# A hybrid attention block on one core: shared transposes of reciprocal sums, values by heads, modulation rows as columns

## The chip, the cores and the metric

The kernel runs on one core of a Trainium2 chip. A core has a matrix engine (TensorE, PE), a vector engine (VectorE, DVE), an activation engine (ScalarE, ACT), GpSimd (POOL), a sync engine (SyncE, SP) that issues all DMAs here, and 16 DMA engines. The metric is the device time of one execution in microseconds (us): the median of several.

## The reference

One layer of a diffusion trunk over 1024 latent tokens (16 rows of 64) and 256 context tokens, width 1024, all in float32. Cut to what matters:

```
m, mc = split(silu(c) @ w_ada + b_ada, 9), split(silu(c_ctx) @ w_ada + b_ada, 9)
x     = x     + 0.5 * m[2]  * rms(swiglu(rms(x)*(1+m[1])+m[0]))        # feed-forward 1
h_ctx = h_ctx + 0.5 * mc[2] * rms(swiglu(...))
qa, ka, va, cq, ckv, kr, gates = split(modnorm(x, m[3], m[4]) @ w_in)  # and of h_ctx
o_na  = neighbourhood_attention(qa, ka, va, ka_ctx, va_ctx, rpb)       # 8 heads of 64, 8x16 windows
q, k, v = up-projections of rms(cq), rms(ckv); rotary on 32 of 96 columns
o_mla = softmax(q k^T / sqrt(96)) v                                    # 8 heads over 1280 keys
y     = sigmoid(gates) * (o_na @ w_o_na, o_mla @ w_o_mla), summed, @ w_out
x     = x + m[5] * rms(y);   x = x + 0.5 * m[8] * rms(swiglu(modnorm(x, m[6], m[7])))
```

## The kernel before

A float32 product is made of three matmuls of two rounded parts: every operand is split into a high half (ScalarE's cast) and a low half (VectorE's subtract), and `mm3` (line 152) sums high x high, high x low and low x high. The feed-forwards and the projections of gates, queries and keys go by *units* (`Unit`): 1024 x 256 of weights against 1024 x 1024 of activations in seven block products of 12 matmuls of 512 columns (the names p3 to p7 in the code), whose sums VectorE makes. The planes of activations are made by `Planes.fill0` and `fill1`: four transposes of 128 x 128 by TensorE, then two ScalarE evictions or one and a VectorE copy, then a VectorE subtract.

The order of work is written out. A `Plan` (line 157) has a list of main steps, mostly one block product each, and side steps hung on them by `spread`; within one slot, side steps run in the order in which they were hung. Every instruction of these parts is kept in this order on its engine. A store is issued some steps after its data (`store`, `flush`), all by SyncE's one queue.

Stages in order of time: the first feed-forward, whose first planes were made without the shift (`shift_planes` adds it later, around 50 us); its down-projection; the normalise chains (`chain1`) and the second set of planes (`fill0s`, from 894 us); the units of gates, queries and keys (to about 1180); the latent projections and the values (`va_tile`, 1262 to 1318), which stores the values for the four column blocks `vws[j]` of the neighbourhood attention; the up-projections (`kv_heads`, with `rotate` for the keys; `q_heads`); then 64 attention *items*: 32 of the neighbourhood attention (head by head, four column blocks each, from 1418 us), 32 of the latent attention (head by head, four blocks of 256 queries, to 1824). Then the merge (`wo_step`), `out_tile` and the second feed-forward. The modulation rows m[2] to m[8] are formed alongside by `AdaSum` (line 271): VectorE multiplies and adds the weights as they arrive, and `add_up` sums the 128 partitions by matmuls with a one-pick column, copies the rows out, and `turn` transposes them into columns.

An item makes scores three items ahead, its softmax (line 1500 or 1598) one or two ahead, then transposes the probabilities (line 150, cast at 1520 or 1622, subtract at 1521 or 1623), and multiplies them with the values (`weigh`). `head_out` (line 1449) ends it: the reciprocals of the sums of exponentials, one column per 128 queries, are spread over 128 columns and transposed by TensorE into rows, ScalarE copies one half of the product (line 1456) and these rows (1457), VectorE adds the other half (1458), and GpSimd multiplies and splits (1459 to 1462).

Of the kernel before, what the change touches and what calls it, by code (L numbers as in the profile page):

```python
# [15 lines left out]
P = 128  # L16
# [27 lines left out]
def hybrid_block(ctx: ExitStack, tc: tile.TileContext, a: dict, out: bass.AP):  # L44
# [98 lines left out]

    vec, act, pool = Engine(nc.vector), Engine(nc.scalar), Engine(nc.gpsimd)
# [12 lines left out]
    class Plan:  # L157
# [113 lines left out]
    class AdaSum(Ada):  # L271
# [30 lines left out]
    def ada_steps(ms):  # L302
# [12 lines left out]
        def end(m):  # L315
            cur[m].turn()
# [5 lines left out]
        for m in ms:  # L322
            s += [lambda m=m, k=k, h=h: step(m, k, h) for k in range(KD + 1) for h in range(2)]
            s += [lambda: None, lambda m=m: cur[m].add_up(), lambda m=m: end(m)]
# [481 lines left out]
    def shift_planes(ks):  # L806
        for k in ks:
# [5 lines left out]
            act.activation(t, t, AF.Identity, bias=mod[0][:, 0, k:k + 1])  # L813
# [203 lines left out]
    def emit_q(i, ci, x, bank):  # L1017
# [11 lines left out]
    def emit_k(i, c0, n, x):  # L1029
        hi, lo = T2(F32R)[:, :n], T2(F32R)[:, :n]  # L1030
        split_to(hi, lo, x)
        store(kas[i][0, :, c0:c0 + n], f32(hi))
        store(kas[i][1, :, c0:c0 + n], f32(lo))

    punits = []
    for p in list(range(4, 12)) + [0, 1, 2, 3]:
# [4 lines left out]
        elif p < 4:  # L1041
            punits.append(Unit(h2, srcs, lambda i, ci, x, bank, i0=i0: emit_k(i0 - 4 + i, ci * 512, 512, x)))
# [6 lines left out]
    plan_chains(plan, pos, 2, chain1)  # L1049

# [4 lines left out]
    plan.spread([lambda k=k: fill0s()[k]() for k in range(KD)], pos[3] + 6, o + 2)  # L1055
# [53 lines left out]
    vws = [DR([4, P, D]) for _ in range(4)]  # L1109
    vcs = DR([NCTX, D])  # L1110
# [51 lines left out]
    def va_tile(s, t):  # L1162
# [5 lines left out]
        if t < 8:  # L1168
            for j in range(4):
                for r in range(2):  # L1170
                    row = 2 * t + r
                    o, q = 64 * r + KSTART[j], (row % 4) * 32
                    store(vws[j][row // 4, q:q + 32, :], f32(v[o:o + 32, :]))
        else:
            store(vcs[(t - 8) * P:(t - 7) * P, :], f32(v))
# [31 lines left out]
    def rotate(x, cc, ss, nh):  # L1207
# [11 lines left out]
        vec.tensor_tensor(x, v1, v2, op=ALU.add)  # L1219

# [54 lines left out]
    class NaHead:  # L1275


        def loads(self, h):
# [15 lines left out]
            for j in range(2):  # L1294
                self.values(va, j)
            yield
            ld(f32(kvc[:, 256:512]).rearrange("p (t c) -> p t c", t=2),
               vcs[:, h * P:(h + 1) * P].rearrange("(t p) c -> p t c", p=P))
# [150 lines left out]
    def head_out(pv, r, h, hi, lo, shape):  # L1449
# [12 lines left out]
        nc.gpsimd.tensor_tensor(lo[b:b + 64], o, f32(hi[b:b + 64]), op=ALU.subtract)  # L1462

# [7 lines left out]
    class NaItem:  # L1471
        def __init__(self, head, j):
            self.head, self.j = head, j

        def scores(self):
# [4 lines left out]
            m, n_, l, r = ST(4), ST(2), ST(2), ST(2)  # L1480
# [17 lines left out]
            self.r = r  # L1498
# [3 lines left out]
            soft.append(lambda: nc.vector.reciprocal(r, l))  # L1502
            yield
# [443 lines left out]
```

## Time and profile before

| | |
|---|---|
| median of 3 runs | 2685.34 us (2684.7 to 2686.59) |
| profiled execution: own time / span | 2686.6 / 2684.8 us |
| granted TensorE clock, mean | 0.996 of full |
| TensorE, VectorE, ScalarE, GpSimd busy | 98%, 69%, 43%, 8% |
| DMA | 409.43 MB, 152 GB/s mean |

A row of a timeline names the engine, the source line (L120 is the helper that pins every instruction, L147 the matmuls, L150 the transposes, L132 the DMAs), the operation and the tiles as out<-in: xu, xv, xy, xo and t are tiles of SBUF, w weights or attention operands, st statistics, bm, bs and bv banks of PSUM, d scratch in HBM, and in_ an input. Where several instructions of one kind follow each other they share a row (x4), and the bracket says how long the engine stood idle before the row and which engine's instruction ended that. A float32 matmul shows as several records where its operands are not rounded ones: one one-column product gives two.

### The profile page before, as it was taken

What the parts mean: (1) busy time and instruction counts of PE and PEld (TensorE: products, weight loads), DVE (VectorE), ACT (ScalarE), POOL (GpSimd) and SP (SyncE); (2) the same over time, 40 slices, a digit from 0 to 9 for tenths busy, and PEclk for the clock granted to TensorE, in tenths of its full rate; (3) what the DMA queues carried; (4) which work ended last, traced back from release to release, by engine and by line L of the source; (5) the groups of instructions that cost most, each with busy time, mean ns of one, the idle gap of its engine ahead of it and who ended that gap; (6) DMA issues with size and microseconds to landing.
All of it is one profiled execution on the core that took longest, in us unless ns stands there. A gap on an engine that the chain in (4) does not pass through costs nothing.

```text
span 2684.8 us, 37871 instructions
## 1 busy us (share of the span) xinstructions
PE 2627.2 (98%) x13820; PEld 2245.7 (84%) x13820; DVE 1845.9 (69%) x3488; ACT 1146.3 (43%) x2176; POOL 218.4 (8%) x348
## 2 busy tenths in 40 slices
PE   7999999999999999999999999999999999999998
PEld 5888888888888788799888999997788888888887
DVE  3777876586876676664558988885445777565776
ACT  5532223522233653331437888882256322324111
POOL 0000000000001300000102422220030000000001
PEclk9999999999999999999999999999999999999999
DMA  7444433453442664486789953205235433225323
GB/s 276 161 154 146 148 122 122 142 168 110 157 134 96 226 208 157 139 294 217 233 274 255 237 124 77 72 9 196 71 118 176 138 130 114 76 90 196 118 94 126
DMA packets 183194, 409.43 MB, mean 152 GB/s; under 512 B 21664, under 2 KB 59744, under 8 KB 183008
## 3 DMA queue, kind: packets, MB, share of 16 engines
q1 hardware_dynamic: 183008, 407.01, 46.9%
q8 instruction: 109, 1.79, 0.3%
q14 instruction: 77, 0.63, 0.1%
HBM read 307.77 MB, written 99.16 MB: 152 GB/s over the span
## 4 chain that ended last, share of the span: by engine, by line
PE 72%; issue 16%; DMA 5%; DVE 3%; ACT 2%; POOL 1%; SPq 0%; DVEq 0%; POOLq 0%; ACTq 0%
PE bs L147 32%; PE bm L147 20%; PE bv L147 16%; DMA w<-d 4%; PE bm L150 3%; DVE t L120 1%; ACT t L120 1%; ACT xu L120 1%; PE bs L150 1%; DVE xv L120 1%; DVE xu L120 1%; POOL st L120 1%; PE bv L150 0%; DMA xv<-in_wada 0%; ACT xv L120 0%
## 5 line engine op out<-in xcount | busy, mean ns | idle before, releaser
L147 PE MATMUL bm<-xu,xu 128*128 128x512 f32 (+2 forms) x2304 | 551.0, 388 | 4.1 <-ACT xu L120 3.3
L147 PEld LDWEIGHTS bm<-xu,xu 128*128 128x128 f32 x2304 | 424.9, 188 | 89.4 <-ACT xu L120 4.1
L147 PE MATMUL bs<-xu,xu 128*128 128x512 f32 (+1 forms) x1908 | 459.0, 386 | 1.4 <-DVE xu L120 0.9
L147 PEld LDWEIGHTS bs<-xu,xu 128*128 128x128 f32 x1908 | 354.1, 189 | 70.5 <-ACT xu L120 0.9
L147 PE MATMUL bs<-xv,xu 128*128 128x512 f32 (+1 forms) x1488 | 352.5, 386 | 3.9 <-DVE t L120 3.9
L147 PEld LDWEIGHTS bs<-xv,xu 128*128 128x128 f32 x1488 | 277.1, 188 | 60.2 <-ACT xu L120 4.6
L147 PE MATMUL bv<-xv,xu 128*128 128x512 f32 x1276 | 318.4, 389 | 0.0
L120 ACT CAST xu<-t 128x512 fp32r<-128x512 f32 x248 | 151.3, 618 | 342.4 <-DVE t L120 333.4
L147 PEld LDWEIGHTS bv<-xv,xu 128*128 128x128 f32 x1276 | 239.5, 188 | 49.7
L120 DVE TENSOR_TENSOR xu<-t,xu 128x512 fp32r<-128x512 f32 x248 | 170.5, 689 | 125.3 <-ACT xu L120 125.3
L120 DVE TENSOR_TENSOR xu<-xv,xu 128x512 fp32r<-128x512 f32 (+2 forms) x244 | 183.0, 770 | 59.8 <-ACT xu L120 56.1
L120 DVE TENSOR_TENSOR xu<-xu,xu 128x512 fp32r<-128x512 f32 (+2 forms) x226 | 155.5, 694 | 84.6 <-ACT xu L120 82.8
L147 PE MATMUL bs<-w,w 96*128 96x512 f32 (+3 forms) x832 | 206.2, 366 | 7.4 <-DMA w<-d 5.6
L120 POOL TENSOR_SCALAR st<-st 128x1 f32<-128x1 f32 x72 | 41.1, 571 | 2098.8 <-ACT t L120 2068.6
L120 ACT CAST xu<-xv 128x512 fp32r<-128x512 f32 (+2 forms) x216 | 137.6, 696 | 125.2 <-DVE xv L120 76.0
L147 PE MATMUL bm<-t,xu 128*128 128x256 f32 (+1 forms) x1272 | 165.9, 288 | 0.6 <-ACT t L120 0.4
L147 PEld LDWEIGHTS bm<-t,xu 128*128 128x128 f32 x1272 | 160.8, 191 | 6.1 <-ACT t L120 0.8
L147 PE MATMUL bv<-xu,xu 128*128 128x512 f32 x596 | 159.6, 390 | 0.0
L147 PE MATMUL bv<-t,w 128*128 128x256 f32 x896 | 148.6, 287 | 1.8 <-DVE t L1623 0.8
L120 ACT CAST xu<-xu 128x512 fp32r<-128x512 f32 (+2 forms) x218 | 132.9, 623 | 29.5 <-DMA xu<-in_wc 23.3
L147 PEld LDWEIGHTS bv<-t,w 128*128 128x128 f32 x896 | 132.7, 189 | 13.8 <-DVE t L1623 1.7
L147 PEld LDWEIGHTS bs<-w,w 96*128 96x128 f32 (+1 forms) x832 | 123.3, 190 | 16.2 <-DVE st L1490 2.8
(181 smaller groups left out, 3675.9 us busy)
## 6 DMA issues: line engine op xcount, KB each, us to landing
d<-t SPq DMA_DIRECT2D x244, 256.0 KB, 2.2
xu<-in_f1w SPq DMA_DIRECT2D x64, 512.0 KB, 4.1
xv<-in_f1w SPq DMA_DIRECT2D x64, 512.0 KB, 3.5
xv<-d SPq DMA_DIRECT2D x62, 512.0 KB, 4.4
xu<-in_f2w SPq DMA_DIRECT2D x60, 512.0 KB, 3.7
t<-in_wada SPq DMA_DIRECT2D x112, 256.0 KB, 3.9
w<-d SPq DMA_DIRECT2D x112, 256.0 KB, 7.1
t<-d SPq DMA_DIRECT2D x76, 256.0 KB, 3.8
```

What stands on the lines that cost most here:

```text
L120: return lambda *x, **y: pin(f(*x, **y))
L147: return pin(nc.tensor.matmul(o, s, m, start=start, stop=stop, skip_group_check=open_group[0]))
L150: return pin(nc.tensor.transpose(o, x, i))
```

## The change

- `shift_planes`: of the two ScalarE ACTIVATEs per plane the second becomes a VectorE TENSOR_SCALAR.
- `AdaSum.end` replaces `add_up` and `turn`: each 128 x 128 piece of the accumulated weights is multiplied with a column of ones, which gives the modulation as columns at once; the step between goes.
- `later`: in the units of queries and keys the low half (VectorE's subtract and its store) is emitted after the side steps of the slot.
- The second `fill0` starts one step earlier, and is hung on before the chains.
- The values are stored as `vws[j][head]`, 128 x 512 each, and `vcs[head]`, so that a load of a head's values is contiguous.
- `rotate_keys` rotates all eight tiles of keys at once, in the value stage, in place of one rotation per tile in `kv_heads`.
- `head_out`: the reciprocals of two items stand in one tile (`sums_of`); GpSimd spreads them over 128 x 256 (`widen`), in space of the rotary table; the even item transposes both halves for itself and its successor, and copies the successor's rows to a tile that is kept (`held`).
- `FirstMerge`: the 24 matmuls of the merge's first output block with the neighbourhood half are issued during the last item and just ahead of the change of pools.

```diff
@@ Plan.run
                 for g in self.side.pop(i, ()):
                     g()
+                while deferred:
+                    deferred.pop(0)()
                 flush(i)
@@ AdaSum
-        def add_up(self):
-            self.bank = PB("v")
+        def end(self):
+            pb = PB("v")
+            n = len(self.acc)
             for v, t in enumerate(self.acc):
-                for g in range(4):
-                    mmul(self.bank[32 * g:32 * g + 32, :256], pick[v], t[g // 2][:, (g % 2) * 256:(g % 2) * 256 + 256],
-                         start=(v == 0), stop=(v == len(self.acc) - 1))
-            self.rows = T2()
-            vec.tensor_copy(self.rows[:, :256], self.bank[:, :256])
+                for k in range(KD):
+                    mmul(pb[:, v * KD + k:v * KD + k + 1], t[k // 4][:, (k % 4) * P:(k % 4 + 1) * P], ones, True, True)
+            for v in range(n):
+                vec.tensor_tensor(mod[self.m][:, v, :], pb[:, v * KD:(v + 1) * KD], bada[:, self.m, :], op=ALU.add)
@@ shift_planes
-            act.activation(t, t, AF.Identity, bias=mod[0][:, 0, k:k + 1])
+            vec.tensor_scalar(t, t, mod[0][:, 0, k:k + 1], None, op0=ALU.add)
@@ emit_q (emit_k alike)
-        vec.tensor_tensor(lv, tv, f32(hv), op=ALU.subtract)
         store(qas[i][0, :, c0:c0 + 512], f32(hi))
-        store(qas[i][1, :, c0:c0 + 512], f32(lo))
+        def low():
+            vec.tensor_tensor(lv, tv, f32(hv), op=ALU.subtract)
+            store(qas[i][1, :, c0:c0 + 512], f32(lo))
+        later(low)
@@ plan of the second planes
-    plan_chains(plan, pos, 2, chain1)
...
-    plan.spread([lambda k=k: fill0s()[k]() for k in range(KD)], pos[3] + 6, o + 2)
+    plan.spread([lambda k=k: fill0s()[k]() for k in range(KD)], pos[3] + 5, o + 1)
+    plan_chains(plan, pos, 2, chain1)
@@ va_tile
-                    store(vws[j][row // 4, q:q + 32, :], f32(v[o:o + 32, :]))
+                    g = (row // 4) * P
+                    store(vws[j][:, q:q + 32, g:g + P].rearrange("h p c -> p h c"),
+                          f32(v[o:o + 32, :]).rearrange("p (h c) -> p h c", h=NH))
@@ NaHead.values
-            ld(f32(v[:, o:o + 512]).rearrange("p (g x) -> p g x", g=4),
-               vws[j][:, :, self.h * P:(self.h + 1) * P].rearrange("g p x -> p g x"))
+            ld(f32(v[:, o:o + 512]), vws[j][self.h])
@@ keys
+    plan.spread([rotate_keys], va_at + 4, va_at + 5)
...
-        for t in tiles_of(ci):
-            if ci < 2:
-                rotate(kr[:, t:t + 1, :], rope[:, t, 0:32], rope[:, t, 32:64], 1)
@@ head_out
-        for i in range(2):
-            turn_(pv[:, 256 + i * P:256 + (i + 1) * P], r[:, i:i + 1].to_broadcast([P, P]), ident)
         b, c = (0, 64) if h % 2 == 0 else (64, 0)
         t = T2()
         o, rb = t[b:b + 64, :256], t[b:b + 64, 256:512]
+        if n % 2 == 0:
+            for i in range(2):
+                turn_(pv[:, 256 + i * P:256 + (i + 1) * P], wide(n)[:, i * P:(i + 1) * P], ident)
+            other = held[0] = T2()
+            nc.scalar.copy(rb, pv[0:64, 256:512])
+            nc.scalar.copy(other[b:b + 64, :256], pv[64:128, 256:512])
+        else:
+            rb = held[0][b:b + 64, :256]
         nc.scalar.copy(o, pv[c:c + 64, :256])
-        nc.scalar.copy(rb, pv[b:b + 64, 256:512])
         nc.vector.tensor_tensor(o, o, pv[b:b + 64, :256], op=ALU.add)
@@ items and merge
+            if n == len(todo) - 1 and x:
+                fm.step(0, (x - 1,))
...
+    fm.step(1, range(4))
...
+        if d + s == 0:
+            pb = fm.pb[ci]
+        else:
```

Three places of the order. First, ScalarE at the shift (xu_226 to xu_229 hold the planes without shift, xu_485 onward the high halves; t_480 and its like are first products, and the CASTs that follow make the next unit's weights). Before:

```order
L120 COPY t_480<-bm_395 128x512
L120 CAST xu_482<-xu_378 128x512
L120 ACTIVATE xu_485<-xu_226,mod_100 128x512
L120 ACTIVATE xu_226<-xu_226,mod_100 128x512
L120 ACTIVATE xu_485<-xu_226,mod_100 128x512
L120 ACTIVATE xu_226<-xu_226,mod_100 128x512
L120 COPY t_509<-bm_496 128x512
```

and now, on ScalarE:

```order
L120 COPY t_480<-bm_395 128x512
L120 CAST xu_482<-xu_378 128x512
L120 ACTIVATE xu_485<-xu_226,mod_100 128x512 x2
L120 COPY t_509<-bm_496 128x512
L120 ACTIVATE xu_486<-xu_227,mod_100 128x512 x2
L120 COPY t_531<-bm_518 128x512
```

and on VectorE, where xu_487 onward are the low halves:

```order
L120 TENSOR_TENSOR xu_482<-xu_378,xu_482 128x512
L120 TENSOR_SCALAR xu_226<-xu_226,mod_100 128x512
L120 TENSOR_TENSOR xu_487<-xu_226,xu_485 128x512
L120 TENSOR_SCALAR xu_226<-xu_226,mod_100 128x512
L120 TENSOR_TENSOR xu_487<-xu_226,xu_485 128x512
L120 TENSOR_SCALAR xu_227<-xu_227,mod_100 128x512
```

Each plane has one ACTIVATE less on ScalarE, and its VectorE subtract has a TENSOR_SCALAR ahead of it that writes what it reads.

Second, VectorE in a query unit (the t that reads a bank, bs or bv, is a block sum; the row that takes two t, one a high half, is the low half of the queries; rows that write xu are low halves of weights). Before:

```order
L120 TENSOR_TENSOR xu_9687<-t_9665,xu_9687 128x512
L120 TENSOR_TENSOR t_9690<-xu_9646,xu_9623 128x512
L120 TENSOR_TENSOR t_9685<-t_9685,bs_9650 128x512
L120 TENSOR_TENSOR t_9710<-t_9685,t_9709 128x512
L120 TENSOR_TENSOR t_9713<-xu_9646,t_9690 128x512
L120 TENSOR_TENSOR xu_9715<-t_9713,xu_9715 128x512
```

and now:

```order
L120 TENSOR_TENSOR t_9580<-xu_9535,xu_9512 128x512
L120 TENSOR_TENSOR t_9575<-t_9575,bs_9540 128x512
L120 TENSOR_TENSOR t_9601<-xu_9535,t_9580 128x512
L120 TENSOR_TENSOR xu_9603<-t_9601,xu_9603 128x512
L120 TENSOR_TENSOR t_9598<-t_9575,t_9597 128x512
L120 TENSOR_TENSOR t_9553<-t_9553,bv_9562 128x512
```

The low half of the queries followed its block sum directly; now two operations on weights stand between.

Third, ScalarE around `head_out` in the neighbourhood attention. Before, over two items:

```order
L1500 ACTIVATE xu_12842,st_12846<-xu_12842,st_12845 128x640
L1500 ACTIVATE xu_12843,st_12846<-xu_12843,st_12845 128x640
L1520 CAST t_12934<-bm_12936 128x512
L1456 COPY t_12959<-bv_12877 64x256
L1457 COPY t_12959<-bv_12877 64x256
L1520 CAST xu_12754<-bm_12966 128x2x128
L1520 CAST t_12977<-bm_12979 128x512
L1500 ACTIVATE xu_12918,st_12922<-xu_12918,st_12921 128x640
L1500 ACTIVATE xu_12919,st_12922<-xu_12919,st_12921 128x640
L1520 CAST t_13004<-bm_13006 128x512
L1520 CAST xu_12751<-bm_13036 128x2x128
L1456 COPY t_13029<-bv_12972 64x256
```

and now, an even and an odd item:

```order
L1549 ACTIVATE xu_12789,st_12793<-xu_12789,st_12792 128x640
L1549 ACTIVATE xu_12790,st_12793<-xu_12790,st_12792 128x640
L1571 CAST t_12881<-bm_12883 128x512
L1571 CAST xu_12701<-bm_12915 128x2x128
L1487 COPY t_12904<-bv_12823 64x256
L1488 COPY t_12907<-bv_12823 64x256
L1491 COPY t_12904<-bv_12823 64x256
L1571 CAST t_12926<-bm_12928 128x512
L1549 ACTIVATE xu_12865,st_12869<-xu_12865,st_12868 128x640
L1571 CAST t_12952<-bm_12954 128x512
L1549 ACTIVATE xu_12866,st_12869<-xu_12866,st_12868 128x640
L1491 COPY t_12975<-bv_12921 64x256
```

Two copies per item became three in the even one, all ahead of VectorE's add, and one in the odd one, which stands behind a softmax of a later item.

## Rows read from the trace of the kernel before

**Rows 1.** The page, parts 1 and 4: busy time, and the chain that ended last.

```profile
PE 2627.2 (98%) x13820; PEld 2245.7 (84%) x13820; DVE 1845.9 (69%) x3488; ACT 1146.3 (43%) x2176; POOL 218.4 (8%) x348
...
PE 72%; issue 16%; DMA 5%; DVE 3%; ACT 2%; POOL 1%; SPq 0%; DVEq 0%; POOLq 0%; ACTq 0%
```

**Rows 2.** Busy time by stretch: stretch, length, each engine, clock, DMA share, GB/s.

```profile
50.00:75.00 25.00, 21.65 (x88) 17.18 (x87) 15.08 (x22) 18.10 (x32) 3.58 (x6) 0.93 0.46 155
...
150.00:200.00 50.00, 50.00 (x222) 41.40 (x222) 37.08 (x59) 14.58 (x25) 0.00 (x0) 1.00 0.38 125
...
875.00:925.00 50.00, 43.86 (x193) 35.05 (x192) 32.35 (x42) 36.06 (x56) 21.27 (x26) 0.93 0.64 224
...
1262.00:1318.00 56.00, 56.00 (x270) 47.03 (x269) 21.16 (x38) 20.45 (x52) 12.35 (x28) 1.00 0.73 229
...
1432.97:1444.73 11.76, 11.76 (x99) 11.76 (x98) 11.00 (x43) 10.95 (x26) 5.48 (x9) 1.00 1.08 246
...
1600.00:1700.00 100.00, 100.00 (x724) 93.72 (x723) 87.39 (x256) 81.85 (x182) 22.40 (x36) 1.00 0.30 74
...
1800.00:1830.00 30.00, 27.07 (x193) 24.26 (x193) 20.58 (x40) 20.37 (x45) 10.00 (x15) 1.00 0.22 73
```

**Rows 3.** What TensorE waited for: total us, times, longest us.

```profile
PE bs L147 <- DMA w<-d: 5.6, 5, 1.6
...
PE bv L150 <- DVE t L120: 2.9, 4, 1.0
...
PE bv L147 <- DVE t L120: 1.4, 2, 1.1
```

**Rows 4.** Timeline of TensorE: start, us, instruction, [idle before <-releaser].

```profile
59.31 4.41 PE L147 MATMUL bm<-xu,xu 128*128 128x512 f32 x10 [3.26 <-ACT xu L120]
...
896.07 0.77 PE L150 MATMUL bs<-ident,xv 128*128 128x128 f32 x5 [0.75 <-ACT xv L120]
...
902.60 0.74 PE L150 MATMUL bs<-ident,xv 128*128 128x128 f32 x4 [2.57 <-ACT xv L120]
...
1113.66 3.00 PE L147 MATMUL bs<-xv,xu 128*128 128x512 f32 x12 [1.77 <-DVE t L120]
...
1129.31 1.40 PE L147 MATMUL bs<-xv,xu 128*128 128x512 f32 x5 [1.77 <-DVE t L120]
...
1358.23 0.65 PE L150 MATMUL bs<-ident,xv 128*128 128x128 f32 x4 [1.49 <-DVE t L120]
...
1825.47 0.70 PE L147 MATMUL bm<-xo,xu 128*128 128x512 f32 x2 [1.52 <-issue]
```

**Rows 5.** Timeline of ScalarE, 52 to 63 us.

```profile
55.91 2.85 ACT L120 ACTIVATE xu<-xu,mod 128x512 fp32r<-128x512 f32 x4
...
58.66 1.13 ACT L120 CAST xu<-xu 128x512 fp32r<-128x512 f32 x2
```

**Rows 6.** Groups of instructions: busy us, mean ns, idle before.

```profile
L120 DVE TENSOR_SCALAR t<-t,sc 128x512 f32<-128x512 f32 x20 | 9.0, 483 | 1.7 <-DMA t<-in_wada 1.7
```

**Rows 7.** Timeline of VectorE in the query units.

```profile
1118.74 0.69 DVE L120 TENSOR_TENSOR t<-t,t 128x512 fp32r<-128x512 f32 x1 [1.35 <-ACT t L120]
```

**Rows 8.** Timeline of TensorE, one-column products and one-pick sums.

```profile
89.95 1.84 PE L147 MATMUL bv<-strip,t 128*128 128x1 f32 x16
...
91.65 0.64 PE L150 MATMUL bs<-ident,xv 128*128 128x128 f32 x4
...
412.41 1.07 PE L147 MATMUL bv<-t,strip 128*32 128x256 f32 x16
```

**Rows 9.** Timeline of VectorE in the key rotation.

```profile
1354.95 0.48 DVE L120 TENSOR_TENSOR t<-kr,rope 128x32 f32<-128x32 f32 x5
```

**Rows 10.** DMA in 127.5:129.5, 175:177 and 1546.3:1547.3, queues full.

```profile
DMA packets 447, 0.81 MB, mean 407 GB/s; under 512 B 50, under 2 KB 50, under 8 KB 447
...
DMA packets 189, 0.68 MB, mean 338 GB/s; under 512 B 23, under 2 KB 23, under 8 KB 189
...
DMA packets 496, 0.25 MB, mean 254 GB/s; under 512 B 0, under 2 KB 496, under 8 KB 496
```

More of the change, by code (lines that the diff above doesn't have):

```diff
@@ L142, in flush, with later @@
             put(*waiting.pop(0)[1:])
+    deferred = []
+    def later(f):
+        deferred.append(f) if clock[0] is not None else f()
     vec, act, pool = Engine(nc.vector), Engine(nc.scalar), Engine(nc.gpsimd)
@@ L315, in end @@
         def end(m):
-            cur[m].turn()
+            cur[m].end()
             if m == 4:
@@ L1024, in emit_q, with emit_k, low @@
         act.copy(hv, tv)
-        vec.tensor_tensor(lv, tv, f32(hv), op=ALU.subtract)
         store(qas[i][0, :, c0:c0 + 512], f32(hi))
-        store(qas[i][1, :, c0:c0 + 512], f32(lo))
-    def emit_k(i, c0, n, x):
+        def low():
+            vec.tensor_tensor(lv, tv, f32(hv), op=ALU.subtract)
+            store(qas[i][1, :, c0:c0 + 512], f32(lo))
+        later(low)
+    def emit_k(i, c0, n, x, bank=True):
         hi, lo = T2(F32R)[:, :n], T2(F32R)[:, :n]
-        split_to(hi, lo, x)
+        act.copy(hi, x)
         store(kas[i][0, :, c0:c0 + n], f32(hi))
-        store(kas[i][1, :, c0:c0 + n], f32(lo))
+        def low():
+            vec.tensor_tensor(lo, x, f32(hi), op=ALU.subtract)
+            store(kas[i][1, :, c0:c0 + n], f32(lo))
+        low() if bank else later(low)
     punits = []
@@ L1107, in htok @@
         return [y[:, (t % 4) * P:(t % 4 + 1) * P] for y in x]
-    vws = [DR([4, P, D]) for _ in range(4)]
-    vcs = DR([NCTX, D])
+    vws = [DR([NH, P, 512]) for _ in range(4)]
+    vcs = DR([NH, P, 256])
     cqs = DR([NLAT, QR])
@@ L1219, in rotate, with rotate_keys @@
         vec.tensor_tensor(x, v1, v2, op=ALU.add)
+    def rotate_keys():
+        t1, t2 = [T2()[:, :256].rearrange("p (t c) -> p t c", t=8) for _ in range(2)]
+        x, cc, ss = kr[:, 0:8, :], rope[:, :, 0:32], rope[:, :, 32:64]
+        vec.tensor_tensor(t1, x, cc, op=ALU.mult)
+        for ax in range(2):
+            for hf in range(2):
+                o, i = ax * 16 + hf * 8, ax * 16 + (1 - hf) * 8
+                vec.tensor_tensor(t2[:, :, o:o + 8], x[:, :, i:i + 8], ss[:, :, o:o + 8], op=ALU.mult)
+        vec.tensor_tensor(x, t1, t2, op=ALU.add)
+    plan.spread([rotate_keys], va_at + 4, va_at + 5)
     qns = [DR([2, P, NLAT]) for _ in range(4)]
@@ L1462, in head_out, with wide, widen, sums_of @@
         nc.gpsimd.tensor_tensor(lo[b:b + 64], o, f32(hi[b:b + 64]), op=ALU.subtract)
+    sums, held = {}, [None]
+    def wide(n):
+        return rope.rearrange("p a b -> p (a b)")[:, (n // 2) % 2 * 256:(n // 2) % 2 * 256 + 256]
+    def widen(n):
+        x = sums[n // 2].rearrange("p (x i o) -> p i x o", i=2, o=1).to_broadcast([P, 2, 2, 64])
+        nc.gpsimd.tensor_copy(wide(n).rearrange("p (i x c) -> p i x c", i=2, x=2), x)
+    def sums_of(n):
+        if n // 2 not in sums:
+            sums[n // 2] = ST(4)
+        return sums[n // 2][:, (n % 2) * 2:(n % 2) * 2 + 2]
     def copy_max(dst, src, m):
@@ L1472, in __init__ @@
         def __init__(self, head, j):
-            self.head, self.j = head, j
+            self.head, self.j, self.n = head, j, 4 * head.h + j
         def scores(self):
@@ L1572, in __init__ @@
         def __init__(self, head, b):
-            self.head, self.b = head, b
+            self.head, self.b, self.n = head, b, 4 * (NH + head.h) + b
         def scores(self):
@@ L1688, in hybrid_block, with load, split, step @@
             soft.pop(0)()
+    class FirstMerge:
+        def load(self):
+            self.r = T2()
+            ld(self.r, a["wo"][0][:, 0:512])
+        def split(self):
+            t = W()
+            self.w = split_to(t[:, 0:512], t[:, 512:1024], self.r)
+            self.pb = [PB("s") for _ in range(2)]
+        def step(self, ci, ks):
+            open_group[0] = True
+            for k in ks:
+                mm3(self.pb[ci], [x[:, k * P:(k + 1) * P] for x in self.w],
+                    [x[:, ci * 512:ci * 512 + 512] for x in ona[k]], k == 0, k == 3)
+            open_group[0] = False
+    fm = FirstMerge()
     for n in range(len(todo)):
         ahead = start(n + AHEAD)
+        if n == len(todo) - 3:
+            fm.load()
+        if n == len(todo) - 2:
+            fm.split()
         parts = started[n].values()
@@ L1730, in wo_step @@
             yt.append(list(zip(*[duo() for _ in range(2)])))
[L1731 to L1734 removed]
+        if d + s == 0:
+            pb = fm.pb[ci]
+        else:
+            pb = PA()
+            w = wos[d][1 + s]
+            for k in range(4):
+                mm3(pb, [x[:, k * P:(k + 1) * P] for x in w], [x[:, c] for x in (ona, omla)[s][k]], k == 0, k == 3)
         z = zt[d, ci, s]
@@ L1745, in hybrid_block @@
     z_load(0)
-    for s in range(2):
-        wo_split(0, s)
+    wos[0].append(None)
+    wo_split(0, 1)
     for d in range(KD):
```

30 lines of the change are left out of this document (14 added, 16 removed).

## Prediction

> **What bounds the kernel now.** I read the busy shares and the chain that ended last first, then stretches of 25 to 100 us, then the list of what TensorE waited for, and only then single starts on the timeline. TensorE is busy for 98% of the span, and the chain runs through it for 72%; "issue" is most of the rest, and DMA holds 5% [rows 1]. In a stretch without gaps 222 matmuls of 512 columns fill 50 us, so one costs 50/222 = 225 ns, and TensorE can't be asked to go faster there [rows 2]. Nothing gains, then, but TensorE instructions that vanish and TensorE idle time that closes. In the two stretches 50:75 and 875:925 TensorE is idle for 3.35 and 6.14 us and its granted clock is .93 (a mean: part of each stretch is at the lower of its two levels, 1.2 instead of 2.4 GHz); in the neighbourhood attention (1432.97:1444.73, three items of 3.92 us) TensorE is full, VectorE and ScalarE have only 0.76 and 0.81 us to spare, and the DMA share is 1.08; in the latent attention (1600:1700) TensorE is full and VectorE at 87% [rows 2]. The 5.6 us in which score matmuls wait for loads (w<-d) are the largest steady wait [rows 3].
>
> The sum is made against the profiled execution: span 2684.8, its own time 2686.6, so 1.8 us lie around the span. It stands 1.26 above the median of the three runs, 2685.34; I take that off at the end.
>
> **The change part by part.**
>
> *Shift planes.* TensorE waits 3.26 us at 59.31 for a CAST on ScalarE [rows 4]. That CAST starts at 58.66 right behind a block of four ACTIVATEs (2.85 us) of the shift, with no idle time between [rows 5]; another such block stands ahead of that one; the 88 matmuls of this stretch need 88 x .225 = 19.8 of 25 us, so 5.2 are lost: 3.35 idle and 1.8 by the lower clock that goes with the wait [rows 2]. The change takes every second ACTIVATE off ScalarE (eight in all) and puts eight TENSOR_SCALARs of .48 [rows 6] on VectorE. In the order ScalarE's CAST then stands behind two instead of four ACTIVATEs per block, about 3 us earlier; VectorE now has 16 operations ahead of the low half of the same weights and is late next: eight pairs, each a scalar and a subtract of .69 that overlap a little, end near 57.6 by my reckoning, and TensorE wants the weights at 59.31 - 3.26 = 56.05. A wait of about 1.2 stays, and the clock may hold: -4.0 (-2.5 if the clock falls all the same, -5.2 if all goes).
>
> *First planes one step earlier.* In 875:925 there are 161 matmuls and 32 transposes of about .11, 39.8 us of work, so 10.2 are lost, 6.14 as idle and the rest by clock [rows 2]. The first transposes already wait .75 for ScalarE's normalise of the fourth tile, the later ones 2.57 [rows 4]. One step is 12 matmuls, 2.7 us: the first transposes will reach their wait that much sooner and stand about 3.4 us there. In return the ScalarE evictions of the planes are emitted ahead of the next chains' squares and normalises, so most of the other 5.4 idle goes. -2.0; between -5 (clock back as well) and +1 (a longer single wait lowers the clock longer).
>
> *Deferred low halves.* The query units make VectorE idle 1.35 each time it waits for ScalarE's high half [rows 7], and TensorE then waits 1.77 for VectorE [rows 4]. Moved behind the next product of the same slot, the subtract no longer waits, but two of the products now wait for a ScalarE cast that stands one copy later, and the number of VectorE operations is the same. The loop per unit is 15.65 us before (1129.31 less 1113.66, both the same wait) and comes out at 15.7 by my count. 0, plus or minus .7.
>
> *Modulation sums as columns.* Before, 80 one-pick matmuls of 256 columns at 1.07/16 = .067 [rows 8] are 5.4 us, seven pairs of transposes at .22 are 1.5, and four waits of TensorE for VectorE's rows (bv<-DVE t: 2.9 and 1.4, one of them before these sums) make some 3.7 [rows 3]: 10.6. After, 3 sums of two vectors take 16 one-column products, 4 of one vector take 8; each product is two records, and 16 such records took 1.70 us from the first to the next instruction [rows 8]: 3 x 3.4 + 4 x 1.7 = 17.0. Their only wait, for the accumulation, goes, because the sums now start a step later. +5.5 (the pairs of starts I could time separately give +5, the two sums above +6.4). The price is that each product loads 128 columns of weights for one column of result. The Trainium skill, "TensorE: Matmul & The Clock Gate", section "Back-to-back issue gap", puts matmuls of 1 to 64 columns at an issue floor of about 25 ns, by which the 160 records would be an estimated 4 us and this edit a gain of some 6; the 106 ns of the row disagree, and its section on LDWEIGHTS (columns over 1.2, 107 ns for 128) agrees with the row.
>
> *Keys rotated once.* TensorE waits 1.49 at 1358.23 for VectorE [rows 4], which stands in 24 small operations of the rotation, .48 for five [rows 9]. The six operations that replace them (8 tiles at once) run in the value stage, where VectorE is busy 21 of 56 us [rows 2]. The shorter waits before it I leave as they are. -1.6 (-1 to -4).
>
> *Value layout and neighbourhood attention.* A head's values are now loaded in runs of 2 KB (1 KB for the context) instead of 512 B. With full queues 512-B packets moved at 254 GB/s, 2-KB ones at 407 [rows 10]; 1.18 MB per head is 4.6 us by the one and 2.9 (3.0 with the context) by the other, 1.6 per head and 13 over eight heads, in a stage whose DMA share is over 1. The 5.6 us of waits for loads can go with it, not more; I take 4. The Trainium skill, "DMA: Bandwidth & Descriptors", section "Specifications", says that line rate is reached from 512 B up; by that nothing of this 4 would come, and the rows disagree. The halved transposes free 16 x .22 = 3.5 us of TensorE here; but per pair of items TensorE then asks 7.62, VectorE 7.33 and ScalarE 7.30, so I take 2.5 of it. The even item's head_out has three ScalarE copies ahead of VectorE's add, the odd one one, before it was two in each: in sum as many, but uneven. -6.5 (-10 to +3).
>
> *Value stores.* The same edit cuts the stores of 1262:1318 from rows of 4 KB into runs of 512 B: 64 stores of 256 packets, 9.4 MB with the context. At 338 GB/s [rows 10] that was 28 us of queue time, at 254 it is 37, +9 where share .73 of 56 us leaves 15. I count 0; the bound is in the second rival.
>
> *Latent attention.* 16 pairs save one pair of transposes each, .22: -3.5, since VectorE has 12.6% to spare [rows 2] (-2 to -3.6). The widening copies are POOL's, which is idle.
>
> *First merge products.* TensorE waits 1.52 at 1825.47 for no recorded event, across the change of pools [rows 4]; with the shorter waits around it 2.93 us are idle in 1800:1830 [rows 2]. 24 matmuls that have to be done anyway (24 x .225 = 5.4 us of work) now fill the gaps of the last item and the change of pools: -2.6 (-1 to -4).
>
> Sum: -4.0 - 2.0 + 0 + 5.5 - 1.6 - 6.5 - 3.5 - 2.6 = -14.7. 2686.6 - 14.7 = 2671.9; less 1.26, **2670.6 us**.
>
> **Rivals.** *1. The neighbourhood attention gains nothing:* what the packets give is taken by VectorE and ScalarE, which are 93% full, and by the uneven copies. For it: those 0.76 us to spare in 11.76. Against: waits for loads, not for VectorE, head the list there. 2670.6 + 6.5 = 2677. The page's 512-B rule leads the same way, with the transposes still gained: 2674.6; chance a tenth of what this rival holds.
> *2. Slower: the value stores overload the queues.* Place: 1262:1365. From about 15 us more of queue time (a 512-B packet 1.16 times as dear as measured on loads: 43 instead of 37 us) the weight loads behind them land late and TensorE waits in the stage after. Were the runs twice as dear as now measured, 74 - 28 = 46 more, 31 beyond the spare 15, less what lies under later work, say 25: 2670.6 + 25 = 2696. For: no row shows a store of such small runs, and the margin is thin. Against: the measured 254 GB/s stays within it.
> *3. The early stalls don't close:* VectorE is as late as ScalarE was, and the longer wait at 892 costs the clock. Shift planes -1, first planes +1, instead of -6: 2676.6.
> *4. The change cancels:* columns cost 6.5, neighbourhood +1, first merge 0: 2686.6 - 4.0 - 2.0 + 6.5 - 1.6 + 1 - 3.5 - 1.3 = 2683.
>
> **How the numbers follow.** The forecast (2664 to 2676 by itself, each term moving by a few us, not all one way) .54; rival 1 .15; rival 3 .11; rival 4 .10; rival 2 .10. Faster by over .2% (5.4 us, about what a measurement of this kernel can tell from no change) means below 2680.0: forecast, rivals 1 and 3 nearly whole, a little of rival 4: .80. Within: rival 4's rest, the tails and the mild cases of rival 2: .12. Slower: .08, the rest of rival 2. The range that leaves out two in ten goes from 2658 (the lower ends of three or four terms together) to 2682.
>
> **What would show it.** Right: one-column records of about .11 on TensorE, 160 of them, and no wait before them; at 56 to 60 a wait under 2 us, for VectorE; near 892 one wait of 3 to 4 us instead of four; no wait for w<-d above 1 us after 1430; 64 instead of 128 transposes from the sums; a latent item pair shorter by .22; no gap at the change of pools. Wrong: DMA share near 1 in 1262:1318 and TensorE waits behind it; neighbourhood items still 3.9 us apart with VectorE the releaser; query loop not near 15.7 us.

## The result: .2% slower, and the profile after

The changed kernel takes 2690.73 us (median of 14 runs) against 2685.93 before (14 runs), a ratio of 1.0019 (95% interval 1.0011 to 1.0027). The profiled execution has a span of 2689.4. TensorE is busy for 11.7 us more than before, with nearly as many instructions, and the chain now holds "issue" (time in which an engine waited for nothing that the profile shows) for a third; the mean granted clock is .994 ([rows 1]; page of the changed kernel, parts 1 and 4):

```profile
PE 2638.9 (98%) x13822; PEld 2259.5 (84%) x13822; DVE 1838.0 (68%) x3443; ACT 1136.2 (42%) x2168; POOL 230.8 (9%) x380
...
PE 52%; issue 33%; ACT 6%; DVE 6%; DMA 2%; POOL 1%; SPq 0%; DVEq 0%; POOLq 0%; ACTq 0%
```

Laid side by side by TensorE's sequence of instructions, the two profiled executions (one of each kernel) part and meet as follows (the same instruction's start after, less its start before; the steps add up to +6.0 at 2669, and the end comes 1.4 earlier behind that):

| stretch of before, us | what is in it | step, us | forecast |
|---|---|---|---|
| 0 to 84 | shift on VectorE | -4.0 (and -0.1 at the start) | -4.0 |
| 404 to 860 | three two-vector modulation sums | +12.7 | +6.3 |
| 860 to 941 | first planes a step earlier | -2.7 | -2.0 |
| 941 to 1163 | query and key units, low halves deferred | +4.8 | 0 |
| 1163 to 1264, and 2570 to 2610 | four one-vector sums | -1.3 and +0.8 | +0.1 |
| 1335 to 1378 | keys rotated once | -3.1 | -1.6 |
| 1378 to 1550 | neighbourhood attention | -0.5 | -6.5 |
| 1550 to 1800 | latent attention | 0.0 | -3.5 |
| 1800 to 1849 | last items, first merge products | -0.5 | -2.6 |

The two forecasts of the sums are by the prediction's prices (3 x 3.4 and 4 x 1.7, less what rows cost there): 6.4 together, of which it took 5.5.

Stretches of the changed kernel, to set beside [rows 2] (columns as there):

```profile
50.00:75.00 25.00, 23.91 (x106) 19.43 (x105) 20.45 (x32) 16.53 (x30) 5.95 (x8) 1.00 0.53 165
424.54:431.37 6.83, 6.83 (x21) 5.67 (x22) 1.36 (x4) 0.00 (x0) 0.00 (x0) 0.50 0.10 38
426.00:430.00 4.00, 4.00 (x11) 3.13 (x12) 0.24 (x2) 0.00 (x0) 0.00 (x0) 0.50 0.01 2
646.41:649.82 3.41, 3.41 (x10) 2.67 (x9) 0.70 (x2) 0.00 (x0) 0.00 (x0) 0.50 0.27 102
789.77:793.18 3.41, 3.41 (x17) 3.41 (x17) 0.24 (x2) 0.00 (x0) 0.00 (x0) 0.50 0.36 133
1121.00:1125.00 4.00, 4.00 (x12) 3.15 (x11) 2.24 (x5) 0.36 (x1) 0.00 (x0) 0.59 0.94 310
1262.00:1318.00 56.00, 56.00 (x269) 47.57 (x269) 20.93 (x42) 17.14 (x46) 12.37 (x28) 1.00 0.90 244
1459.00:1475.70 16.70, 15.77 (x124) 15.07 (x123) 15.63 (x57) 14.84 (x37) 8.19 (x14) 1.00 1.05 255
1600.00:1700.00 100.00, 99.78 (x714) 92.44 (x713) 84.69 (x253) 79.90 (x180) 24.71 (x42) 1.00 0.29 74
```

In 50:75 the clock is 1.00 where it was .93. In 426:430 TensorE has 11 matmuls of 512 columns in 4 us and a clock of .50, the lower of its two levels, and in 1121:1125 12 at .59; at full clock 4 us hold 18. The three stretches at .50 around the two-vector sums are 13.65 us together; at half speed that loses an estimated 6.8 us, about what the sums cost beyond their forecast. Its timeline, which answers to [rows 4] and [rows 8]:

```profile
57.50 6.19 PE L153 MATMUL bm<-xu,xu 128*128 128x512 f32 x26 [1.09 <-DVE xu L120]
...
421.80 4.31 PE L153 MATMUL bv<-strip,t 128*128 128x1 f32 x32
425.97 5.47 PE L153 MATMUL bm<-xu,xu 128*128 128x512 f32 x12
431.24 3.00 PE L153 MATMUL bs<-xv,xu 128*128 128x512 f32 x12
...
904.61 0.76 PE L156 MATMUL bs<-ident,xv 128*128 128x128 f32 x5 [3.46 <-ACT xv L120]
...
1120.20 4.57 PE L153 MATMUL bs<-xv,xu 128*128 128x512 f32 x12 [1.89 <-DVE t L120]
...
1137.54 1.71 PE L153 MATMUL bs<-xv,xu 128*128 128x512 f32 x4 [1.84 <-DVE t L120]
```

The 32 records of one column take 4.17 us up to the next instruction, and the 12 matmuls behind them 5.27, where 12 at full clock take 2.72. Behind each of the two waits in the query units, 1.89 and 1.84 long, 12 matmuls take 4.4 us; behind the waits of 1.77 in [rows 4] they took 2.84. So a good part of the loss is TensorE itself at its lower clock, which no list of waits shows: it counts as busy time.

### The profile page after: what moved, and what is told of

Same layout as the page of the kernel before. It is cut to its first block, busy times and chain, and to the rows that moved or that the text cites. A ratio compares the mean times of both kernels' runs of the same rounds, so it can differ in the third digit from the quotient of the medians.

```text
span 2689.4 us, 37823 instructions
## 1 busy us (share of the span) xinstructions
PE 2638.9 (98%) x13822; PEld 2259.5 (84%) x13822; DVE 1838.0 (68%) x3443; ACT 1136.2 (42%) x2168; POOL 230.8 (9%) x380
## 4 chain that ended last, share of the span: by engine, by line
PE 52%; issue 33%; ACT 6%; DVE 6%; DMA 2%; POOL 1%; SPq 0%; DVEq 0%; POOLq 0%; ACTq 0%
PE bs L153 23%; PE bm L153 15%; PE bv L153 11%; PE bm L156 2%; ACT xu L1648 1%; DVE t L120 1%; DVE xu L1515 1%; DVE xu L120 1%; ACT xu L1549 1%; POOL st L120 1%; DVE xv L120 1%; ACT t L120 1%; ACT t L1674 1%; DVE t L1675 1%; ACT xu L120 1%
## 5 line engine op out<-in xcount | busy, mean ns | idle before, releaser
L153 PEld LDWEIGHTS bv<-t,w 128*128 128x128 f32 x896 | 132.6, 189 | 20.6 <-DVE t L1675 5.0
```

The costliest lines, as they stand in the source:

```text
L153: return pin(nc.tensor.matmul(o, s, m, start=start, stop=stop, skip_group_check=open_group[0]))
```

## Experiments

All are the changed kernel with the edit shown; each was timed beside the kernel before (whose medians there are 2685.7 to 2686.7). Ratios are to the kernel before, where the changed one has 1.0019.

**The modulation sums by rows again (e1_rows).**

```diff
-            for v, t in enumerate(self.acc):
-                for k in range(KD):
-                    mmul(pb[:, v * KD + k:v * KD + k + 1], t[k // 4][:, (k % 4) * P:(k % 4 + 1) * P], ones, True, True)
+            # add_up() and turn() of the kernel before
```

> The changed kernel, with the modulation sums as before (one-pick sums of rows, copied and transposed). Theory C (the granted TensorE clock falls to its lower level in and behind the long rows of one-column products, so that each of the three two-vector sums costs the 3.5 us of its records and some 3 more in the 12 matmuls behind it): 2690.7 - 12 = about 2679, and the granted clock around these three sums is 1.00 again. Rival P (a one-column record costs its .11 us and nothing else): 2690.7 - 5.5 = about 2685.

Measured: 2680.32, ratio .9978 (.9969 to .9987), 10.4 less than the changed kernel. That is nearer to theory C than to P, whose 5.5 it nearly doubles. The granted clock around the three sums is 1.00 again (e1_rows, the first of them):

```profile
400.00:430.00 30.00, 30.00 (x146) 24.09 (x145) 18.81 (x33) 8.41 (x16) 0.00 (x0) 1.00 0.20 70
```

**The same columns in four parts (e2_spread).**

```diff
-        s += [lambda: None] * 2 + [lambda m=m: end(m)]
+        s += [lambda: None] * 2 + [lambda m=m, x=x: cur[m].part(x, 4) for x in range(3)] + [lambda m=m: end(m)]
```

> The changed kernel, with the same one-column products in four parts, each behind another main step, so that blocks of large matmuls stand between them. Theory C: the clock holds, the 6.5 us beyond the price of the records go, about 2684. Rival P: no change, 2690.7 plus or minus 1.

Measured: 2685.59, ratio .9996 (.9987 to 1.0006), 5.1 less. The same 32 records, eight at a time between main steps, cost .81 per eight and nothing behind them (e2_spread, TensorE; and the clock there):

```profile
415.23 0.95 PE L154 MATMUL bv<-strip,t 128*128 128x1 f32 x8
416.04 3.03 PE L154 MATMUL bv<-xv,xu 128*128 128x512 f32 x12
```

```profile
414.00:418.00 4.00, 4.00 (x24) 3.40 (x23) 1.36 (x3) 0.62 (x1) 0.00 (x0) 1.00 0.25 76
418.00:422.00 4.00, 4.00 (x19) 3.33 (x18) 2.07 (x4) 0.00 (x0) 0.00 (x0) 1.00 0.76 247
```

All 21 rows of 32 records, three in each of the seven profiles that have them (the changed kernel's among them), were followed by 12 instructions that took 0.9 to 2.5 us more than their price; none of 48 rows of 16 records was, and none of the rows of eight. P falls: the records' price is real (3.5 per sum), but the clock took some 6.4 more in the three sums together (+12.7 for +6.3 in the table of the steps).

**Low halves at once (e3_nolater, and e12_defer the other way round).**

```diff
     def later(f):
-        deferred.append(f) if clock[0] is not None else f()
+        f()
```

> The changed kernel, with the low halves of queries and keys emitted at once, as before. Theory C (the wait of TensorE in the query units is as long as before within .15 us, but falls so that the clock goes to its lower level twice, some 1.7 us each): 2690.7 - 3.5 to - 5 = about 2686.5. Rival (the query units cost the same either way, and the 5 us there come from where the units begin): 2690.7, the two falls of the clock near 1121 and 1138 still there.

Measured: 2689.03, ratio 1.0010 (1.0001 to 1.0018), 1.7 less, between the two forecasts; the interval overlaps the changed kernel's, so the time alone doesn't settle it. In its trace both waits are back at 1.76 and no clock falls there. The same question on the quieter version e8_best (below, which emits the low halves at once):

> The version measured at 2674.5 with the low halves of queries and keys deferred again. Theory C: the two waits in the query units each make the clock fall, 3.4 us, and one wait of 1.0 near 990 comes back: 2678 to 2679. Rival (deferral costs nothing): 2674.5.

Measured: 2678.19, ratio .9971 (.9961 to .9982), 3.7 more than e8_best; all eight runs (2676.58 to 2680.06) lie above e8_best's five (2672.72 to 2675.14). TensorE in e8_best, at the second wait of the query units, and then in e12_defer, at both (where the answer ends, 10 matmuls have taken 2.55 us in the one and nine 3.54 in the other):

```profile
1122.84 2.55 PE L153 MATMUL bs<-xv,xu 128*128 128x512 f32 x10 [1.76 <-DVE t L120]
```

```profile
1107.19 3.00 PE L153 MATMUL bs<-xv,xu 128*128 128x512 f32 x12 [1.89 <-DVE t L120]
...
1122.96 3.54 PE L153 MATMUL bs<-xv,xu 128*128 128x512 f32 x9 [1.88 <-DVE t L120]
```

A wait of 1.76 leaves the clock alone; one of 1.88 lets it fall behind the second but not behind the first here. Over all profiles: 14 such waits without deferral, no fall; 18 with it, 14 falls of 1.6 us each. So the deferral brings the falls, and all it does to TensorE at these two places, as far as the traces show, is to lengthen the wait by about a tenth of a microsecond. That the length alone decides isn't shown: four of the 18 waits, as long as the others, left the clock alone, and so did a wait of 1.80 in the neighbourhood attention in four of the 15 profiles that have it (in the changed kernel, first, and not in e8_best; the wait, then the stretch with the clock):

```profile
1429.35 1.80 PE L153 MATMUL bs<-w,w 128*128 128x256 f32 x8 [1.80 <-DVE st L1540]
```

```profile
1428.00:1436.00 8.00, 4.82 (x28) 3.87 (x28) 5.51 (x25) 5.16 (x13) 0.40 (x1) 1.00 1.05 230
```

```profile
1414.01 2.23 PE L153 MATMUL bs<-w,w 128*128 128x256 f32 x7 [1.81 <-DVE st L1535]
```

```profile
1412.00:1420.00 8.00, 5.73 (x28) 4.94 (x26) 4.14 (x22) 4.89 (x13) 0.00 (x0) 0.79 1.05 229
```

**Each item's own transposes (e4_ownhead).**

```diff
-        if n % 2 == 0:
-            (transposes for two items; three copies)
+        r = sums_of(n)
+        for i in range(2):
+            turn_(pv[:, 256 + i * P:256 + (i + 1) * P], r[:, i:i + 1].to_broadcast([P, P]), ident)
```

> The changed kernel, with each item again transposing its own reciprocals (64 more pairs of TensorE transposes of .22 each at 32 items of each kind, in all 32 pairs more) and two ScalarE copies per item; the values stay laid by heads. Theory H (what the shared transposes free on TensorE is lost to ScalarE and VectorE: three copies ahead of one add, and an odd item's softmax steps two at once): the same or a little faster, 2686 to 2691. Rival (the transposes saved are time saved): 32 x .22 = 7 us slower, 2697.7.

The expectation's "64 more pairs" is a slip for 32. Measured: 2689.03, ratio 1.0008 (.9999 to 1.0017): with 32 more pairs of transposes the kernel is 1.7 faster, if anything. They were not time saved. In the traces the neighbourhood attention takes 126.2 us with them and 126.7 in the changed kernel, the latent attention 256.9 and 256.8; the clock falls in neither.

**Even steps in the softmax (e5_pops), and the copies in another order (e6_copies).**

```diff
-            soft.append(total)
-            if self.n % 2:
-                soft.append(lambda: widen(self.n))
+            soft.append(total)                       # which calls widen itself
```

> The changed kernel, with the spreading copy put into the same softmax step as the reciprocal, so that an odd item has as many steps as an even one and its two exponentials are no longer emitted next to each other. Theory H1 (the odd item's doubled step is what delays ScalarE): 2 to 4 us faster, most of it in the latent attention. Theory H2 (the three copies ahead of the even item's add are): within 1 us of 2690.7.

Measured: 2688.7, ratio 1.0014 (1.0005 to 1.0022), 2.0 less. But in its profile two falls of the clock that didn't come, near 906 and 1120, make 1.6 each, more than the whole; the neighbourhood attention is .6 shorter and the latent attention .3 longer: inconclusive for H1 by the time, against it where the gain was looked for.

```diff
+            nc.scalar.copy(o, pv[c:c + 64, :256])
+            nc.vector.tensor_tensor(o, o, pv[b:b + 64, :256], op=ALU.add)
             nc.scalar.copy(... pv[0:64, 256:512])
             nc.scalar.copy(... pv[64:128, 256:512])
-        nc.scalar.copy(o, pv[c:c + 64, :256])
-        nc.vector.tensor_tensor(o, o, pv[b:b + 64, :256], op=ALU.add)
```

> The changed kernel, with the even item's copy of its product first, VectorE's add behind it, and the two copies of reciprocals after that, in a tile of their own. H2: VectorE's add waits for one copy instead of three, 2 to 4 us faster. H1: within 1 us of 2690.7.

Measured: 2701.43, ratio 1.0061 (1.0049 to 1.0074), 10.7 more: a miss for both. ScalarE's second copy now waits for VectorE's add, which itself waits its turn on VectorE; both attention stages grew (133.0 and 258.1 us, against 126.7 and 256.8) and so did their end. The row shows the new wait; how the 10.7 divides was not taken apart:

```profile
1659.58 0.37 ACT L1487 COPY t<-bv 64x256 f32<-64x256 f32 x1
...
1660.64 0.36 ACT L1489 COPY t<-bv 64x256 f32<-64x256 f32 x1 [0.19 <-DVE t L1488]
```

**The values as before (e7_oldlayout).** The stores of 32 rows of 4 KB and the loads in runs of 512 B of the kernel before.

> The changed kernel, with the values stored and loaded as before (rows of 4 KB out, runs of 512 B in). Theory V (in the neighbourhood attention TensorE waits for the ring of VectorE and ScalarE, and the waits for loads of before only stood in the place of these): within 1.5 us of 2690.7, the waits at the heads' starts again put down to loads. Rival D (the layout does save the 4 to 5.6 us of waits for loads, and something else takes them elsewhere): 2695 or more.

Measured: 2690.69, ratio 1.0016 (1.0007 to 1.0025), the changed kernel's time. V holds. TensorE's waits at the heads' starts in e7_oldlayout and in the changed kernel (columns as in [rows 3]):

```profile
PE bs L153 <- DVE st L1539: 5.3, 7, 1.8
...
PE bs L153 <- DMA w<-d: 0.6, 1, 0.6
```

```profile
PE bs L153 <- DVE st L1540: 7.1, 8, 1.8
```

But for one of .6 they are VectorE's in both, which V had not expected of the old layout: with the rest of the change in place, the loads are no longer last even in the old layout. Either way the stage takes about the same (127.3 us, with a fall of the clock in it, and 126.7 without one). With each item's own transposes as before and the new layout (e8_best, below), the waits for VectorE come to 5.7, what the loads' were in [rows 3]: those stood where VectorE and ScalarE would have made TensorE wait anyway.

**The three failed parts undone (e8_best), and the one-vector sums as columns (e11_cols1).** e8_best joins the edits of e1_rows, e3_nolater and e4_ownhead; e11_cols1 sums by columns only where there is one vector:

```diff
+            s += [lambda: None, lambda m=m: cur[m].add_up() if m < 5 else None, lambda m=m: end(m)]
```

> The changed kernel with three of its parts as before: modulation sums by rows, low halves at once, and each item's own transposes; kept are the shift on VectorE, the first planes a step earlier, the keys' rotation at once, the value layout and the first merge products. If the parts add (-11, -3, -2 by the runs on their own): about 2675, faster than the kernel before by .4%. If they don't (waits that take each other's place): 2678 to 2681.

> The version measured at 2674.5, but with the four one-vector modulation sums as columns (16 records each) and the three two-vector sums by rows. Theory C: rows of 16 records don't lower the clock, and the waits of rows (some 1.3 each in three of the four) go for about 1.0 more of records each: 2673.5, within 1 us of 2674.5. If 16 records lower it too: 2677 or more.

Measured: e8_best 2674.53, ratio .9956 (.9942 to .9969); e11_cols1 2673.51, ratio .9953 (.9941 to .9966). Both beat both kernels. The parts add, and a little more: on their own the three runs gave 10.4, 1.7 and 1.7 less, 13.8 together (the expectation put 3 for the second), and joined they give 16.2. The two don't differ beyond noise, but their profiles do as expected: -1.3 in 1163:1264 and +0.8 at the last sum, and no fall behind 16 records:

```profile
1207.62 1.84 PE L153 MATMUL bv<-strip,t 128*128 128x1 f32 x16
1209.33 2.19 PE L153 MATMUL bs<-xv,xv 128*128 128x352 f32 x12
```

**Where the shared transposes lose what they free (e9_late, e10_sharelate, e13_twocopies, e14_share).** e9_late emits the third copy behind the next part's cast; e10_sharelate does that, and e5_pops' edit, on e8_best's base; e14_share is e8_best with the shared transposes as in the changed kernel; e13_twocopies is that without the third copy.

```diff
-            nc.scalar.copy(other[b:b + 64, :256], pv[64:128, 256:512])
+            late.append(lambda: nc.scalar.copy(other[b:b + 64, :256], pv[64:128, 256:512]))   # e9, e10
+            (left out; the odd item reads the even one's rows)                               # e13
```

> The changed kernel, with the third ScalarE copy of an even item (the reciprocals for its successor) emitted behind the next part's cast instead of ahead of VectorE's add; the bank is held that much longer. H2 (three copies in a row delay the casts and VectorE's subtracts behind them, and that takes the 7 us that the shared transposes free): 3 to 5 us faster than 2690.7, most of it in the latent attention. Rival (the attention stages are set by ScalarE and VectorE as a whole, not by this row of copies): within 1 us.

> The version measured at 2674.5 (sums by rows, low halves at once), but with shared transposes, the third copy late and the spreading copy in the reciprocal's step. H1 and H2 together: 2670 to 2672, the saved transposes at last come through. Rival: 2674 to 2677.

> The version measured at 2674.5 with shared transposes, but the third ScalarE copy of an even item left out: the odd item multiplies with its predecessor's reciprocals (part of the computation is changed, two copies per even item and one per odd one remain). H2 (the third copy delays the cast and the subtract behind it, and one wait of .19 per pair in the latent attention eats the .22 that the transposes free): the latent attention takes 253.5 to 255 us instead of 256.9, the whole 2671 to 2673. Rival (something else there, such as VectorE's own row of work, holds the stage at 256.9): 2674 to 2677, and the wait of .19 per pair is still there.

> The version measured at 2674.5 with shared transposes as in the changed kernel, three copies and all. By the traces so far the latent attention takes 256.8, as with own transposes, and the end of the items 1 to 2 us more: 2675 to 2677.

Measured: e9_late 2694.8, ratio 1.0034 (1.0021 to 1.0046), against H2; e10_sharelate 2677.42, .9968 (.9955 to .9980), against H1 and H2 together; e13_twocopies 2673.47, .9949 (.9935 to .9962), between the two forecasts; e14_share 2676.39, .9961 (.9949 to .9974), as forecast. By stage, from the traces (first to last score product of a stage):

| us | before | changed | e8_best | e14_share | e13_twocopies | e9_late |
|---|---|---|---|---|---|---|
| neighbourhood attention | 127.0 | 126.7 | 126.9 | 127.2 | 125.8 | 129.4 |
| latent attention | 256.9 | 256.8 | 256.9 | 256.8 | 255.9 | 255.9 |
| its end, to the merge's next product | 20.6 | 25.3 | 23.9 | 28.0 | 26.3 | 28.0 |

(All but before have 5.4 us of the merge's products inside the last row.) Part of these differences is the clock. Behind the wait of 1.8 shown above it fell in e8_best, e14_share, e13_twocopies and e9_late, which by that row is 1.7 us of their neighbourhood attention (.21 x 8), and not in the first two columns. And at the end of the items e14_share has it at .69 for 11 us, 3.4 of its 28.0, and e13_twocopies at .84, 1.8 of its 26.3, where e8_best and the changed kernel have 1.00 (e14_share, then e8_best):

```profile
1800.00:1811.00 11.00, 9.41 (x50) 8.67 (x51) 6.64 (x13) 7.42 (x16) 4.01 (x7) 0.69 0.23 89
```

```profile
1800.00:1811.00 11.00, 10.19 (x77) 9.29 (x77) 8.46 (x16) 8.99 (x19) 3.72 (x6) 1.00 0.01 4
```

The latent attention itself has no fall. There the .22 per pair come back in one place: one group of four value products takes at most .49 us from its start to the next instruction in every pair of e8_best; in e14_share and the changed kernel it does so in the first four pairs and the last, and takes .64 to .89 in the eleven between. That is 2.9 us more, of the 16 x .22 = 3.5 that the transposes free; the other value products are the same within .02. In the changed kernel one such group is the row at 1652.22, .67 long against .48 of its like; ScalarE's casts ahead of it stand behind the three copies, and VectorE's subtract behind those (the last fence is the same group in e8_best, .49 long):

```profile
1650.60 0.64 PE L153 MATMUL bv<-t,w 128*128 128x256 f32 x4
...
1652.22 0.84 PE L153 MATMUL bv<-t,w 128*128 128x256 f32 x4
1652.89 0.60 PE L156 MATMUL bm<-ident,xu 128*128 128x128 f32 x4
```

```profile
1650.04 0.35 ACT L1487 COPY t<-bv 64x256 f32<-64x256 f32 x1
1650.40 0.37 ACT L1488 COPY t<-bv 64x256 f32<-64x256 f32 x1
1650.68 0.37 ACT L1491 COPY t<-bv 64x256 f32<-64x256 f32 x1
1651.07 0.59 ACT L1674 CAST t<-bm 128x512 fp32r<-128x512 f32 x1
```

```profile
1651.08 0.41 DVE L1492 TENSOR_TENSOR t<-t,bv 64x256 f32<-64x256 f32 x1 [0.76 <-ACT t L1491]
1651.69 0.69 DVE L1675 TENSOR_TENSOR t<-bm,t 128x512 fp32r<-128x512 f32 x1 [0.20 <-ACT t L1674]
```

```profile
1671.33 0.65 PE L153 MATMUL bv<-t,w 128*128 128x256 f32 x4
1671.82 0.60 PE L156 MATMUL bm<-ident,xu 128*128 128x128 f32 x4
```

Without the third copy (e13_twocopies) the group takes .63 to .65 in those eleven pairs, another one grows from .48 to .53, and the stage is .8 us shorter. So the third copy holds about a quarter of the 3.5. What holds the rest stays open: with two copies left in the even item and one in the odd, the value products still wait there, and neither emitting the copy later (e9_late, where the stage takes the same 255.9) nor leaving it out brings the 3.5 us back.

## Why the prediction was wrong

It said 2670.6, with a range of 2658 to 2682, and the time is 2690.7. Four steps failed: the price of the modulation sums, that of the deferred low halves, and the gains in the two stages of attention. Step by step:

- *Shift planes*: right, in mechanism and size (-4.0), the wait for VectorE included (1.09 at 57.50), and the clock held (1.00 in 50:75).
- *First planes*: right in size (-2.7 for -2.0), in part by luck. The long wait came as forecast (3.46 at 904.61), but of the other waits 1.46 at 924.85 and .29 stayed; in all the idle time shrank by only .9. The rest is the clock, which the prediction left out of its -2.0: before, it was at the lower level for 6.83 us here, and behind the longer wait for 3.41, so a longer wait did not lower it longer, as the prediction's upper bound has it (before, then now). In the 15 profiles with the longer wait it was 3.41 in ten, 6.83 in four, and in one the clock held:

```profile
903.04:909.87 6.83, 6.24 (x19) 4.66 (x17) 5.12 (x10) 3.88 (x7) 0.66 (x1) 0.50 0.76 270
```

```profile
905.82:909.23 3.41, 3.41 (x10) 2.67 (x9) 2.37 (x5) 2.29 (x4) 0.55 (x1) 0.50 0.38 154
```

- *Modulation sums*: the step that puts 160 records at .11 each, 17.0 us against 10.6 before, failed. The records cost about what was said, 3.5 per two-vector sum where the clock held. But the sum took TensorE's clock as given while TensorE does one column of work per weight load; it fell at each of the three sums, and the term was +12.2 instead of +5.5. The prediction put the clock into its terms where TensorE waits, and not where it is busy with nothing but weight loads. (The Trainium skill, "TensorE: Matmul & The Clock Gate", section "Back-to-back issue gap", gives the 25 ns for a matmul by itself and counts the weight load as well in a stream of loads and matmuls, so it doesn't contradict the row's 106 ns, as the prediction has it.)
- *Deferred low halves*: the loop "comes out at 15.7 by my count", so 0, failed. The count of the loop was right: 15.77 where the clock held (e2_spread, from 1116.69 to 1132.46), the waits grown from 1.77 to 1.89. What failed is that so small a difference was priced at its own length; with it the clock fell in 14 of 18 cases, twice here (3.2 of the +4.8), and a wait at 995.65 grew from .31 to .89 besides.
- *Neighbourhood attention*: "the 5.6 us of waits for loads can go with it": they went, and VectorE's took their place in full (-0.5 for -6.5); with the old layout the time is the same (e7_oldlayout), and the 2.5 for the transposes didn't come either (e4_ownhead). Rival 1, given .15, is what happened here, at the place and for the reason named as far as VectorE goes: it is 94% busy in 1459:1475.7 and ends the waits. How much of it is the uneven copies was not taken apart.
- *Latent attention*: "-3.5, since VectorE has 12.6% to spare" failed: 0.0. A mean share to spare says nothing of the one place where the value products wait for VectorE's subtract, behind an even item's three copies; the third copy is about a quarter of it (e13_twocopies), and what the rest is stays open.
- *Keys*: right, larger (-3.1), since two of the shorter waits ahead of it, .46 and .49, which the prediction left as they were, went as well. *First merge products*: -0.5 in the changed kernel, because with shared transposes the last items wait for ScalarE (1.11 at 1818.73; .63 with two copies, no such wait with own transposes); -1.7 in e8_best, nearer the -2.6 of the forecast.
- *Value stores*: rival 2 did not come. DMA share in 1262:1318 rose from .73 to .90, 9.5 us of queue time for the +9 that was counted, and TensorE had no gap there.

No rival of the prediction had the clock fall behind busy TensorE time. (Rival 4's own terms come to 2681.7, not to the 2683 that stands there.) With 6.7 more for the sums, 4.8 for the deferred low halves, and 6.0 and 3.5 less from the two stages of attention, its own sum is -14.7 + 6.7 + 4.8 + 6.0 + 3.5 = +6.3; the steps measured make +6.0. The other misses (first planes -0.7, keys -1.5, last items +2.1) cancel by luck.

## What to carry to other kernels

Where TensorE is the bound, price an edit by what TensorE's clock does behind it: long rows of tiny products count as busy and still let it fall, and a wait can be longer by a tenth of a microsecond and cost 1.6 us. Split such rows among large products, and keep the longest waits as short as they were. A stage's length in one trace can hold a fall of the clock that another trace lacks, so read the clock of a stage before its length is put down to an edit. And instructions taken off the bounding engine gain only if nothing in the same ring got longer: count what the others have in a row at the worst place, not their mean share.

## What was not expected of the hardware

- 32 records of one column in a row (3.5 to 4.7 us) were followed by matmuls at the lower clock in 21 cases of 21; 16 records (1.7 us) in none of 48, and eight between large products in none of 12.
- Behind TensorE waits of 1.76 to 1.77 in the query units the clock stayed in 14 of 14, behind waits of 1.84 to 1.89 it fell in 14 of 18. Behind the wait of 1.80 early in the neighbourhood attention it fell in 11 of 15.
- Splitting the value stores into runs of 512 B put 18468 packets for 4425 through the queues in 56 us, and the share rose from .73 to .90 only: 244 GB/s against 229.
